# A later place for the merge steps of the next head, and a fixed place in ScalarE's queue for the spread of the inverses

## The chip, the cores and the metric

The kernel runs on one core of one Trainium2 chip. The metric is the device time of one execution in microseconds (us). The engines of the core are TensorE (PE in the profile; PEld is its loading of weights), VectorE (DVE), ScalarE (ACT), GpSimd (POOL) and SyncE (SP). SP issues nearly all the DMAs; each engine takes its own instructions strictly in the order of its queue, so an instruction that waits holds up all that stand behind it.

## The reference

The reference is one layer of a hybrid diffusion backbone: 512 latent tokens and 256 context tokens of 1024 channels go through adaptive normalization, one combined input projection, two token mixers side by side (a bidirectional gated DeltaNet with 8 heads and a bidirectional mLSTM with 4 heads), a gated merge, an output projection, and a gated MLP with a 3x3 convolution. The change touches the DeltaNet alone. Its core is

```
kb = k * beta[..., None]
a_strict = jnp.einsum('bhnld,bhnsd->bhnls', kb, k) * decay
rhs = jnp.concatenate([v * beta[..., None], kb * jnp.exp(gc)[..., None]], axis=-1)
sol = lax.linalg.triangular_solve(a_strict, rhs, left_side=True, lower=True, unit_diagonal=True)
...
def step(s, xc):
    u_n, w_n, kt_n, gt_n = xc[:4]
    v_new = u_n - jnp.einsum('bhld,bhde->bhle', w_n, s)
    s_next = s * gt_n[..., None, None] + jnp.einsum('bhld,bhle->bhde', kt_n, v_new)
    ...
    o = jnp.einsum('bhld,bhde->bhle', qd_n, s) + jnp.einsum('bhls,bhse->bhle', at_n, v_new)
```

For each head, direction and chunk of tokens a triangular system is solved, and then a state of 128x128 is carried from chunk to chunk. The output of a head is normalized over its channels and gated.

## The kernel before, in words

The kernel works with chunks of 128 tokens, so that a head has six chunks (two of context, four of latent tokens) in two directions, which makes twelve triangular matrices. For each it forms the inverse explicitly, and the scan then only multiplies.

**A head passes three stages.** `gdn_prep` projects k, q, v and z of the head (L113 and L114 are the matmuls of all projections), convolves them, forms the triangular matrices (pkk on TensorE, L704 on VectorE) and calls `inverses`. That inverts the 16x16 blocks on the diagonals: the blocks are gathered into cd (L766, L767), written to DRAM and read back in another layout (L768, L769), inverted on GpSimd by a chain of 28 small instructions (L778, L780), written to DRAM again (L782) and read back as cx (L783). L783 waits for L782 to land, and L782 for the last step of the chain.

`merges` builds the whole 128x128 inverse out of these blocks in seven steps, each ended by a `yield`:

1. two DMAs for the decay of the queries (L796), each followed by a product with q on GpSimd (L797; the results are called qs_0 and qs_1); the spread of cx into a block-diagonal U by two ScalarE instructions (L805); a transpose of U on VectorE (L806)
2. y0p, 48 small matmuls (L812), and its copy (L814)
3. w0p (L819), the sum (L821), and eight copies on ScalarE (L823, L825) with eight transposes on VectorE (L824, L826)
4. y1p (L844) and its copy (L846)
5. wp (L852), copies on ScalarE (L856), transposes on VectorE (L857)
6. y2p (L865) and its copy on ScalarE (L867)
7. w2p (L873) and its copies on VectorE (L877)

`gdn_scan` then runs the six chunks of both directions side by side. A chunk has p1 (L911), X (L915, VectorE), p2 (L919), the eviction v3 on ScalarE (L927), p3 (L931) and the new state S (L938, VectorE); in the latent chunks an eviction v2 (L944) and the outputs into a PSUM bank called po (L902) are added. A scan has 16 `yield`s. `gdn_tail` normalizes a finished head: squares of po (L958, ScalarE), a sum (L960), a power on GpSimd that makes the scale fo (L961), and the eviction of po through that scale into o (L964, ScalarE). The bank po is cleared for the next scan by a matmul with zeros (L897), which has to wait until L964 has read it.

**What sets the order.** `mixers` runs the scans s = 0 to 11 (eight DeltaNet heads, four of the mLSTM). At every yield of scan s, `drive` issues what belongs beside it: steps of the tail of head s-1 at the yields in TAIL, the merge steps of head s+1 at the yields in MERGE, and as much of the preparation of a later head as SHARE allots. The framework's scheduler then forms each engine's queue from the order in which the program issues the work, and from its own model of durations. On top of that, `follow(ins, key)` ties an instruction behind the one that `self.anchor[key]` holds at that moment; the keys in use are "t" (matmuls of the scan), "v" (its VectorE work) and "p" (the chain on GpSimd).

Of the kernel before, what the change touches and what calls it, by code (L numbers as in the profile page):

```python
# [12 lines left out]
AF = mybir.ActivationFunctionType  # L13
# [47 lines left out]
LATER = 400  # L61
UP = (0, 9, 13)
XN = 7
MERGE = (1, 2, 4, 6, 8, 10, 11)

DBG = None

# [1 line left out]
class Kern:  # L69
# [716 lines left out]
    def merges(self, h):  # L786

        nc, rot, hold = self.nc, self.rot, self.hold
# [13 lines left out]

        U, UT = (self.gx[:, 2 * G1 + 256 + 384 * i : 2 * G1 + 640 + 384 * i].rearrange("p (c i) -> p c i", i=32) for i in range(2))
        for i in range(2):
            nc.scalar.activation(U[:, :, 16 * i : 16 * i + 16], cx, AF.Copy, scale=self.pm[:, i : i + 1])  # L805
        nc.vector.transpose(UT.rearrange("p c i -> p (c i)"), U.rearrange("p c i -> p (c i)"))  # L806
        yield
        y0p = self.pt([P, NB, 32], "mg", f"y0p{h}")
# [78 lines left out]
    def gdn_scan(self, h):  # L887

        nc = self.nc
        hold, rot, small, tmp = self.hold, self.rot, self.small, self.tmp  # L890
        kT, qT, zs, kt, vt, sc, ssq, Tt, at, _ = self.st[h]
        qs = self.qs[h]
        po = self.pt([P, XC, P], "po", f"po{h}")
        self.po[h] = po
        S = [None, None]
        self.left = 4 * XC
        nc.tensor.matmul(po, self.zero, self.zero.unsqueeze(1).broadcast_to([P, XC, P]), start=True, stop=False)  # L897
        order = [list(range(NCH)), list(range(CC - 1, -1, -1)) + list(range(NCH - 1, CC - 1, -1))]

        def out(x, a, b):  # L900
            self.left -= 1
            nc.tensor.matmul(po[:, x, :], a, b, start=False, stop=self.left == 0)  # L902

        for st in range(NCH):
            cs = [order[d][st] for d in range(2)]
            first = st == 0
            X = [vt[:, c, :] for c in cs]
            if not first:
                p1 = self.pt([P, 2, P], "sc", f"p1_{h}")
                for d, c in enumerate(cs):  # L910
                    g = nc.tensor.matmul(p1[:, d, :], kT[:, c * P : c * P + P], S[d], start=True, stop=True)  # L911
                self.anchor["t"] = g
                for d, c in enumerate(cs):
                    X[d] = tmp.tile([P, P], F32, tag="X", name=f"X{h}")
                    self.anchor["v"] = nc.vector.scalar_tensor_tensor(X[d], p1[:, d, :], self.colA[:, c, 2 + d, h : h + 1], vt[:, c, :], ALU.mult, ALU.subtract)  # L915
                yield
            p2 = self.pt([P, 2, P], "sc", f"p2_{h}")
            for d, c in enumerate(cs):
                g = nc.tensor.matmul(p2[:, d, :], Tt[d][:, c, :], X[d], start=True, stop=True)  # L919
            self.anchor["t"] = g  # L920
            j = 0 if first else 1
            Sn = [None, None]
            if st < NCH - 1:
                v3 = []
                for d, c in enumerate(cs):
                    v3.append(tmp.tile([P, P], F32, tag="v", name=f"v3_{h}", bufs=3))
                    nc.scalar.activation(v3[d], p2[:, d, :], AF.Copy, scale=sc[d][:, 2 + j, c : c + 1])  # L927
                yield
                p3 = self.pt([P, 2, P], "sc", f"p3_{h}")
                for d, c in enumerate(cs):  # L930
                    g = nc.tensor.matmul(p3[:, d, :], kt[:, c, :], v3[d], start=True, stop=True)  # L931
                self.anchor["t"] = g
                for d, c in enumerate(cs):
                    Sn[d] = rot.tile([P, P], F32, tag=f"S{d}", name=f"S{h}_{d}", bufs=2)
                    if first:
                        g = nc.vector.tensor_copy(Sn[d], p3[:, d, :])
                    else:
                        g = nc.vector.scalar_tensor_tensor(Sn[d], S[d], self.ge[:, d, h, c : c + 1], p3[:, d, :], ALU.mult, ALU.add)  # L938
                    self.anchor["v"] = g
            if cs[0] >= CC:  # L940
                for d, c in enumerate(cs):
                    x = c - CC
                    v2 = tmp.tile([P, P], F32, tag="v", name=f"v2_{h}", bufs=3)
                    nc.scalar.activation(v2, p2[:, d, :], AF.Copy, scale=sc[d][:, j, c : c + 1])  # L944
                    out(x, qs[d][:, x * P : x * P + P], S[d])
                    out(x, at[d][:, x, :], v2)
            S = Sn
            yield
# [210 lines left out]
    def mixers(self, e_hc, l1):  # L1159
# [20 lines left out]
        for s in range(GH + MH):  # L1180
# [4 lines left out]
            if s + 1 < GH:  # L1185
                side.append((self.merges(s + 1), MERGE))
            if s in (GH - 1, GH):
# [349 lines left out]
```

## Time and profile before

| | |
|---|---|
| time, median of three runs | 1409.82 us (1408.49 to 1412.16) |
| profiled execution, its time | 1413.52 us |
| profiled execution, its span | 1411.6 us |
| mean granted clock of TensorE | 0.966 |
| TensorE busy | 1326.0 us, 94% |
| VectorE, ScalarE, GpSimd busy | 908.5, 588.5, 507.8 us |
| scans of the eight DeltaNet heads | about 188 to 680 us of the span |

The page of the profile gives for each group of instructions its line, engine, operation, tiles (out<-in), shape, count and times, and the idle time of its engine just before it with the instruction that ended it. A timeline row reads: start, duration, engine, line, operation, tiles, count, and in brackets the idle time before and its releaser. SPq stands for a DMA's issue on SP. Granted clock 1.00 is full speed.

The first L919 with the tile vt is taken as the start of a scan. The starts of scans 0 to 7 lie at 187.79, 249.61, 307.09, 365.47, 425.58, 482.69, 544.55 and 611.50 us.

### The profile page before, as it was taken

What the parts mean: (1) busy time and instruction counts of PE and PEld (TensorE: products, weight loads), DVE (VectorE), ACT (ScalarE), POOL (GpSimd) and SP (SyncE); (2) the same over time, 40 slices, a digit from 0 to 9 for tenths busy, and PEclk for the clock granted to TensorE, in tenths of its full rate; (3) what the DMA queues carried; (4) which work ended last, traced back from release to release, by engine and by line L of the source; (5) the groups of instructions that cost most, each with busy time, mean ns of one, the idle gap of its engine ahead of it and who ended that gap; (6) DMA issues with size and microseconds to landing.
All of it is one profiled execution on the core that took longest, in us unless ns stands there. A gap on an engine that the chain in (4) does not pass through costs nothing. (4 is left out here: it accounts for less than half of the span.)

```text
span 1411.6 us, 24202 instructions
## 1 busy us (share of the span) xinstructions
PE 1326.0 (94%) x9436; PEld 1121.7 (79%) x9436; DVE 908.5 (64%) x1860; ACT 588.5 (42%) x1283; POOL 507.8 (36%) x626
## 2 busy tenths in 40 slices
PE   5888699999999999999899999999989999999997
PEld 4777588878887887889788877788878888888886
DVE  6748973748575774655654464644559879879933
ACT  6555554545555554323233334432234333333331
POOL 4426131130321303243735662000135555555552
PEclk9999799999999999999999999999989999999999
DMA  8633233231322322354524442364323333233321
GB/s 244 152 88 93 56 80 83 74 102 37 89 77 69 82 50 77 106 151 117 144 75 112 114 118 61 98 202 139 126 69 111 90 98 102 84 104 90 104 90 60
DMA packets 233232, 141.85 MB, mean 100 GB/s; under 512 B 32977, under 2 KB 215518, under 8 KB 233118
## 3 DMA queue, kind: packets, MB, share of 16 engines
q1 hardware_dynamic: 233118, 140.31, 35.3%
q8 instruction: 74, 1.21, 0.4%
q14 instruction: 40, 0.33, 0.1%
HBM read 134.47 MB, written 5.82 MB: 99 GB/s over the span
## 5 line engine op out<-in xcount | busy, mean ns | idle before, releaser
L1507 DVE SCALAR_TENSOR_TENSOR y<-pu,fw,y 128x441 f32<-128x441 f32 (+2 forms) x352 | 230.0, 691 | 38.5 <-ACT y L1498 32.9
L137 POOL TENSOR_TENSOR rs<-pw_t,mhalf 128x1 f32<-128x1 f32 x14 | 8.2, 584 | 168.3 <-DVE pw_t L136 168.3
L137 POOL TENSOR_TENSOR kh<-pw_t,phalf 128x6 f32<-128x6 f32 x8 | 11.1, 1390 | 124.1 <-DVE pw_t L136 124.1
L293 POOL TENSOR_TENSOR aw<-aw,sc 128x512 f32<-128x512 f32 x32 | 40.0, 1256 | 31.1 <-DMA aw<-in_w_ada_dram 31.0
L915 DVE SCALAR_TENSOR_TENSOR X<-p,colA,vt 128x128 f32<-128x128 f32 x80 | 24.3, 346 | 33.9 <-PE p L911 33.7
L797 POOL TENSOR_TENSOR qs<-qs,qT 128x512 f32<-128x512 f32 x16 | 20.8, 1304 | 62.2 <-DMA qs<-gd 50.1
L773 POOL MEMSET gx<- 96x16 f32 x8 | 1.0, 123 | 115.4 <-DMA gx<-scr 115.4
L927 ACT ACTIVATE v<-p,sc 128x128 f32<-128x128 f32 x80 | 25.4, 367 | 34.4 <-PE p L919 34.3
L931 PE MATMUL p<-v,kt 128*128 128x128 f32 x160 | 29.8, 302 | 10.5 <-ACT v L927 10.5
L778 POOL TENSOR_TENSOR iv_t<-gx 96x14 f32<-96x14 f32 (+6 forms) x112 | 36.0, 322 | 7.5
L1076 DVE SCALAR_TENSOR_TENSOR C<-C,ge,mpc 128x257 f32<-128x257 f32 x32 | 15.3, 479 | 36.3 <-PE mpc L1072 36.2
L780 POOL TENSOR_TENSOR gx<-gx,iv_t 96x14 f32<-96x14 f32 (+6 forms) x112 | 34.8, 311 | 8.6
L1498 ACT ACTIVATE y<-pu,fw 128x512 f32<-128x512 f32 x44 | 30.0, 683 | 16.1 <-PE pu L114 6.8
L931 PEld LDWEIGHTS p<-v,kt 128*128 128x128 f32 x160 | 23.0, 195 | 16.8 <-ACT v L927 14.9
L646 DVE SCALAR_TENSOR_TENSOR Eg<-Eg,colA,mask 128x128 f32<-128x128 f32 x96 | 33.1, 411 | 3.9 <-DMA Eg<-gd 3.9
L1449 POOL TENSOR_TENSOR al<-y,ah 128x512 fp32r<-128x512 f32 x22 | 28.7, 1304 | 17.3 <-ACT ah L1448 15.8
L1281 DVE SCALAR_TENSOR_TENSOR x<-x,py 128x512 f32<-128x512 f32 x16 | 11.0, 686 | 36.6 <-PE py L114 36.6
L938 DVE SCALAR_TENSOR_TENSOR S<-S,ge,p 128x128 f32<-128x128 f32 x64 | 19.3, 343 | 18.2 <-PE p L931 17.1
L911 PE MATMUL p<-S,kT 128*128 128x128 f32 x160 | 29.9, 289 | 0.0
L944 ACT ACTIVATE v<-p,sc 128x128 f32<-128x128 f32 x64 | 23.1, 378 | 15.8 <-PE p L931 15.0
L1459 DVE TENSOR_TENSOR fd_t<-pd,m 128x512 f32<-128x512 f32 x8 | 5.3, 685 | 37.5 <-PE pd L114 37.5
L598 ACT ACTIVATE cv_t<-cv_y 128x512 f32<-128x512 f32 (+1 forms) x40 | 21.8, 546 | 17.2 <-DVE cv_y L597 14.2
(1235 smaller groups left out, 4699.4 us busy)
## 6 DMA issues: line engine op xcount, KB each, us to landing
aw<-in_w_ada_dram SPq DMA_DIRECT2D x41, 256.0 KB
uw<-in_w_ada_dram SPq DMA_DIRECT2D x16, 512.0 KB
Eg<-gd SPq DMA_DIRECT2D x16, 384.0 KB
gx<-in_w_ada_dram SPq DMA_DIRECT2D x23, 256.0 KB
qs<-gd SPq DMA_DIRECT2D x16, 256.0 KB
xn<-in_x_dram SPq DMA_DIRECT2D x4, 512.0 KB
Em<-r1d SPq DMA_DIRECT2D x8, 256.0 KB
mwo_0r<-in_w_in_dram SPq DMA_DIRECT2D x4, 512.0 KB
```

The costliest lines, as they stand in the source:

```text
L293: eng.tensor_tensor(w, w, self.sc[:, 4 * i : 4 * i + 4, 0:1].broadcast_to([P, 4, P]), ALU.mult)
L646: self.follow(nc.vector.scalar_tensor_tensor(E[:, c, :], E[:, c, :], self.colA[:, c, d, row : row + 1], self.mask[d], ALU.add, ALU.min), "v")
L778: eng.tensor_tensor(t, Bi[:, 0:j, j : j + 1].broadcast_to([8 * NB, j, n]), Bi[:, j : j + 1, j + 1 :].broadcast_to([8 * NB, j, n]), ALU.mult)
L780: g = eng.tensor_tensor(Bi[:, 0:j, j + 1 :], Bi[:, 0:j, j + 1 :], t, ALU.add)
L911: g = nc.tensor.matmul(p1[:, d, :], kT[:, c * P : c * P + P], S[d], start=True, stop=True)
L915: self.anchor["v"] = nc.vector.scalar_tensor_tensor(X[d], p1[:, d, :], self.colA[:, c, 2 + d, h : h + 1], vt[:, c, :], ALU.mult, ALU.subtract)
L927: nc.scalar.activation(v3[d], p2[:, d, :], AF.Copy, scale=sc[d][:, 2 + j, c : c + 1])
L931: g = nc.tensor.matmul(p3[:, d, :], kt[:, c, :], v3[d], start=True, stop=True)
L944: nc.scalar.activation(v2, p2[:, d, :], AF.Copy, scale=sc[d][:, j, c : c + 1])
L1449: nc.gpsimd.tensor_tensor(al[:, j, :], ys[0], ah[:, j, :].bitcast(F32), ALU.subtract)
L1498: nc.scalar.activation(y, ps, AF.Copy, scale=tap(0, 0))
L1507: g = nc.vector.scalar_tensor_tensor(o, u3[:, r0 + dy : r1 + dy, c0 + dx : c1 + dx], tap(dy, dx), o, ALU.mult, ALU.add)
```

## The change

Two edits. MERGE moves the seven merge steps of the next head: the first six each by two yields (from 1, 2, 4, 6, 8, 10 to 3, 4, 6, 8, 10, 12) and the last from 11 to 13. And the two ScalarE instructions that spread the inverses (L805) are tied behind the latest v3 eviction that the scan has issued by then; for this the eviction L927 sets an anchor with the new key "s". The first head's merges run before any scan and have no anchor. The work itself, its instructions and their sizes, is the same.

```diff
-MERGE = (1, 2, 4, 6, 8, 10, 11)
+MERGE = (3, 4, 6, 8, 10, 12, 13)
...
         for i in range(2):
-            nc.scalar.activation(U[:, :, 16 * i : 16 * i + 16], cx, AF.Copy, scale=self.pm[:, i : i + 1])
+            self.follow(nc.scalar.activation(U[:, :, 16 * i : 16 * i + 16], cx, AF.Copy, scale=self.pm[:, i : i + 1]), "s")
...
                     v3.append(tmp.tile([P, P], F32, tag="v", name=f"v3_{h}", bufs=3))
-                    nc.scalar.activation(v3[d], p2[:, d, :], AF.Copy, scale=sc[d][:, 2 + j, c : c + 1])
+                    self.anchor["s"] = nc.scalar.activation(v3[d], p2[:, d, :], AF.Copy, scale=sc[d][:, 2 + j, c : c + 1])
```

On ScalarE at the start of scan 2, before. Here gx is U, cdx holds the inverses, v_2 is the v3 of scan 2, junk with sso the squares of po, Eg a decay table:

```order
L1250 ACTIVATE ge_5_3651<-px_g_5_3658 128x512
L805 ACTIVATE gx<-cdx_3324,pm 128x12x16 x2
L739 ACTIVATE junk,ssq_3641<-ps_tm_q_3636 128x128
L927 ACTIVATE v_2_3702<-p_2_3699,sc_0_2154 128x128
L927 ACTIVATE v_2_3704<-p_2_3699,sc_1_2159 128x128
L739 ACTIVATE junk,ssq_3641<-ps_tm_q_3636 128x128 x2
L958 ACTIVATE junk,sso_3733<-po_2884 128x128 x4
L595 ACTIVATE cv_y<-pc_k_3713,cw 128x256
L964 ACTIVATE o_3745<-po_2884,fo_3742 128x128 x4
```

The same place after the change:

```order
L927 ACTIVATE v_2_3702<-p_2_3699,sc_0_2154 128x128
L927 ACTIVATE v_2_3704<-p_2_3699,sc_1_2159 128x128
L739 ACTIVATE junk,ssq_3641<-ps_tm_q_3636 128x128
L958 ACTIVATE junk,sso_3733<-po_2884 128x128 x4
L595 ACTIVATE cv_y<-pc_k_3713,cw 128x256
L964 ACTIVATE o_3745<-po_2884,fo_3742 128x128 x4
L647 ACTIVATE Eg_0_3776<-Eg_0_3776 128x768
L927 ACTIVATE v_2_3816<-p_2_3813,sc_0_2154 128x128
L927 ACTIVATE v_2_3818<-p_2_3813,sc_1_2159 128x128
L805 ACTIVATE gx<-cdx_3297,pm 128x12x16 x2
```

L805 has gone from ahead of the first pair of v3 to behind the second pair, past the evictions of o. In scans 4 and 6 it is the same; in scans 3 and 5 it stood between L595 and L964 before, and now also stands behind the second pair.

On GpSimd at the end of the inverse chain, around the start of scan 3, before. gx<-gx,iv_t are steps of the chain, qs the decayed queries, fo the scale of o:

```order
L780 TENSOR_TENSOR gx<-gx,iv_t 96x4x11
L797 TENSOR_TENSOR qs_1_3753<-qs_1_3753,qT_3165 128x512
L778 TENSOR_TENSOR iv_t<-gx 96x36
L780 TENSOR_TENSOR gx<-gx,iv_t 96x3x12
L778 TENSOR_TENSOR iv_t<-gx 96x26
L780 TENSOR_TENSOR gx<-gx,iv_t 96x2x13
L778 TENSOR_TENSOR iv_t<-gx 96x14
L780 TENSOR_TENSOR gx<-gx,iv_t 96x14
L797 TENSOR_TENSOR qs_0_4529<-qs_0_4529,qT_3978 128x512
L961 TENSOR_TENSOR fo_4521<-fo_4521,mhalf 128x4
```

And after the change:

```order
L780 TENSOR_TENSOR gx<-gx,iv_t 96x4x11
L778 TENSOR_TENSOR iv_t<-gx 96x36
L780 TENSOR_TENSOR gx<-gx,iv_t 96x3x12
L778 TENSOR_TENSOR iv_t<-gx 96x26
L780 TENSOR_TENSOR gx<-gx,iv_t 96x2x13
L778 TENSOR_TENSOR iv_t<-gx 96x14
L780 TENSOR_TENSOR gx<-gx,iv_t 96x14
L797 TENSOR_TENSOR qs_1_3823<-qs_1_3823,qT_3099 128x512
L797 TENSOR_TENSOR qs_0_4599<-qs_0_4599,qT_3912 128x512
L961 TENSOR_TENSOR fo_4521<-fo_4521,mhalf 128x4
```

The product for qs_1 has left the chain and stands behind its last step; L961 stands behind both products, as it stood behind the one. SP's queue at this place had the DMAs of qs_0, L782 and L783 in this order in scans 3 and 5, and has L782, qs_0, L783 now; in scans 2, 4 and 6 qs_0 stands behind L783 both times.

On VectorE at the end of the preparation, in scan 2, the rows around L767 before:

```order
L713 TENSOR_TENSOR at_1_4205<-pqk_4198,Eg_1_3838 128x512
L766 TENSOR_SCALAR cdx_4138<-cg_4137,pm 128x192
L599 SCALAR_TENSOR_TENSOR vT_4247<-cv_t,cv_y 128x256
L767 SCALAR_TENSOR_TENSOR cdx_4138<-cg_4137,pm,cdx_4138 128x192
L772 MEMSET cg_4137 128x12x16
```

and after the change:

```order
L713 TENSOR_TENSOR at_1_4178<-pqk_4171,Eg_1_3778 128x512
L766 TENSOR_SCALAR cdx_4111<-cg_4110,pm 128x192
L857 STREAM_TRANSPOSE Dm<-gx 32x6x32 x4
L599 SCALAR_TENSOR_TENSOR vT_4214<-cv_t,cv_y 128x256
L767 SCALAR_TENSOR_TENSOR cdx_4111<-cg_4110,pm,cdx_4111 128x192
L772 MEMSET cg_4110 128x12x16
```

The four transposes of merge step 5 have come between the two instructions that fill cd. Before, they stood ahead of the whole group, ahead of L704.

## The prediction

> **What bounds the kernel now.** I read the page first, then TensorE's waits in the part where the eight DeltaNet scans run, then the timelines around the starts of two scans.
>
> ```profile
> span 1411.6 us, 24202 instructions
> PE 1326.0 (94%) x9436; PEld 1121.7 (79%) x9436; DVE 908.5 (64%) x1860; ACT 588.5 (42%) x1283; POOL 507.8 (36%) x626
> ...
> PE p L931 <- ACT v L927: 10.5, 6, 3.3
> PE po L897 <- ACT o L964: 2.7, 2, 1.6
> ```
>
> TensorE works 94% of the span, so the end is set by the amount of its work, by its gaps and by its granted clock. The change alters no matrix product; it can win only gaps and clock. Between 130 and 560 us (the last two rows: total, times, longest) there are six waits of L931 for the eviction v3 (L927) and two of L897 for o (L964), 13.2 us in all; they stand at the start of scans 0 and 2 to 6. The even scans 2, 4 and 6 look like this (scan 2, which starts at 307.09):
>
> ```profile
> 307.25 0.32 SPq L782 DMA_DIRECT2D scx<-gx  x1
> 309.40 0.67 SPq L796 DMA_DIRECT2D qs<-gd  x1
> 311.74 0.80 ACT L805 ACTIVATE gx<-cdx,pm 128x192 f32<-128x192 f32 x2 [3.32 <-DMA cdx<-scx]
> 313.10 0.79 PE L931 MATMUL p<-v,kt 128*128 128x128 f32 x2 [3.30 <-ACT v L927]
> 313.54 1.26 POOL L797 TENSOR_TENSOR qs<-qs,qT 128x512 f32<-128x512 f32 x1 [6.32 <-DMA qs<-gd]
> 318.16 1.13 ACT L964 ACTIVATE o<-po,fo 128x128 f32<-128x128 f32 x4
> 323.86 0.39 PE L897 MATMUL po<-zero 128*128 128x512 bf16 x1
> ```
>
> The spread of the inverses (L805) is ahead of the scan's first v3 in ScalarE's queue and waits for a DMA, and v3 (L927) runs behind it, and TensorE waits 3.30 us at L931. In scans 3 and 5 the same L805 stands one place later, ahead of o (scan 3, start 365.47):
>
> ```profile
> 365.47 0.61 PE L919 MATMUL p<-vt,gx 128*128 128x128 f32 x4
> 368.48 0.33 SPq L796 DMA_DIRECT2D qs<-gd  x1
> 371.25 0.32 SPq L782 DMA_DIRECT2D scx<-gx  x1
> 371.84 1.29 POOL L797 TENSOR_TENSOR qs<-qs,qT 128x512 f32<-128x512 f32 x1 [0.62 <-DMA qs<-gd]
> 373.10 1.06 POOL L961 TENSOR_TENSOR fo<-fo,mhalf 128x4 f32<-128x4 f32 x1
> 375.41 0.80 ACT L805 ACTIVATE gx<-cdx,pm 128x192 f32<-128x192 f32 x2 [3.67 <-DMA cdx<-scx]
> 376.12 1.12 ACT L964 ACTIVATE o<-po,fo 128x128 f32<-128x128 f32 x4
> 377.29 0.38 PE L897 MATMUL po<-zero 128*128 128x512 bf16 x1 [1.55 <-ACT o L964]
> 378.28 0.74 PE L931 MATMUL p<-v,kt 128*128 128x128 f32 x4 [0.61 <-ACT v L927]
> ```
>
> After a gap the clock is often granted low for a while. Columns: window, its length, TensorE busy, granted clock, DMA share, GB/s.
>
> ```profile
> 312.00:318.00 6.00, 4.90 (x62) 0.50 0.45 135
> 376.00:382.00 6.00, 4.09 (x19) 1.00 0.01 3
> 431.00:435.00 4.00, 3.77 (x43) 0.57 0.68 210
> 494.00:500.00 6.00, 5.28 (x17) 0.72 0.00 0
> 549.00:555.00 6.00, 5.54 (x116) 0.72 0.44 137
> ```
>
> Busy time times what the clock lacks is 2.45 us in scan 2, 0 in scan 3, 1.6 in scan 4, 1.5 in scan 5, 1.55 in scan 6: about 7 us. With the 13.2 us of idle time, **about 20 us hang on these starts**; that is the most that can be won.
>
> **The change, part by part.** (1) *L805 goes behind the second pair of v3.* In the even scans the first L931 finds its v3 at once. In scan 0, whose gap is quoted next, that is the whole effect.
>
> ```profile
> 190.97 0.49 PE L931 MATMUL p<-v,kt 128*128 128x128 f32 x2 [0.79 <-ACT v L927]
> 431.23 0.65 PE L931 MATMUL p<-v,kt 128*128 128x128 f32 x2 [2.94 <-ACT v L927]
> 494.11 0.38 PE L897 MATMUL po<-zero 128*128 128x512 bf16 x1 [1.17 <-ACT o L964]
> 549.46 0.49 PE L931 MATMUL p<-v,kt 128*128 128x128 f32 x2 [2.20 <-ACT v L927]
> ```
>
> What is late next is o. TensorE's own work from the scan's start to L897 is 10.3 us in scan 3 (377.29 less 1.55, from 365.47). For scan 2 I estimate 9 us, since its L897 stands at 323.86, and the 16.8 us from the start hold 3.3 idle, the block y0p, which now comes later (about 2 us), and some 2.5 lost to the clock. Until now scan 2's head gap hid that o comes late: L964 ran only at 318.16. In the changed order o hangs on POOL: L961, which computes o's scale, stands behind the two products with qs (L797), and these stand behind the last step of the inverse chain.
>
> (2) *The merge steps stand two yields later.* So qs_1's product, which used to run inside the inverse chain, three steps before its end, comes after it. This takes one product of 1.3 us out of the chain. Against it the chain starts later: the four transposes L857 now stand between L766 and L767, which feeds the chain, and VectorE is without a gap there; and ScalarE's eight copies L823 and L825 now run after the third v3, ahead of the norms of the next head.
>
> ```profile
> 276.49 1.57 DVE L857 STREAM_TRANSPOSE Dm<-gx 32x192 f32<-32x192 f32 x4
> 326.84 0.36 ACT L823 COPY gx<-gx 32x192 f32<-32x192 f32 x1 [2.17 <-DVE gx L821]
> 328.96 0.34 ACT L825 COPY Dm<-gx 32x192 f32<-32x192 f32 x1
> 335.96 1.04 ACT L102 CAST wz4h<-wz4r 128x1024 fp32r<-128x1024 f32 x1 [0.82 <-PE px_q L113]
> ```
>
> The transposes cost 1.57 us. The copies take 2.5 us (326.84 to 329.30); 0.82 of that fits into ScalarE's idle time before L102, and 1.3 us of L856's copies leave the same stretch, so 0.4 us is left. 1.57 + 0.4 - 1.3: **the chain ends about 0.7 us later** against its scan. Its bounds: -1.3 (if the later start is hidden) and +2 (if the copies find no idle time).
>
> (3) *The qs DMAs.* In scans 3 and 5 the one for qs_0 is now queued on SP behind L782, which waits for the chain's end; before, it was issued 2.8 us ahead of it. In the even scans it stands behind L783 as before.
>
> *Even scans.* From L782 to the end of o: 2.15 us until the DMA's issue (309.40 - 307.25), 4.14 to the product (313.54 - 309.40), 1.26, then L961 1.06 and L964 1.12: 9.7 us. L782 stood at +0.16, -0.15 and -0.82 us from the scan's start, its first L919 (rows of scans 4, 6 and 5 below); 0.7 later, o ends at 10.6, 10.3 and 9.6 us after the start, against TensorE's arrival at about 9. So it waits 1.6, 1.3 and 0.6 us at L897, and then 0.6 each at L931 as in scan 3, since Eg (L647) and the second v3 follow o on ScalarE: 5.3 us in place of 3.30 + 2.94 + 2.20 = 8.4. Gain 3.1 us. The clock: the split gap of scan 5 (1.17 + 0.6) cost 1.5, that of scan 3 none; I take 1 us each, 3 in place of 5.6. Gain 2.6.
>
> ```profile
> 425.43 0.32 SPq L782 DMA_DIRECT2D scx<-gx  x1
> 425.58 0.38 PE L919 MATMUL p<-vt,Bt 128*128 128x128 f32 x2
> 543.73 0.32 SPq L782 DMA_DIRECT2D scx<-gx  x1
> 544.55 0.38 PE L919 MATMUL p<-vt,gx 128*128 128x128 f32 x2
> 482.69 0.50 PE L919 MATMUL p<-vt,gx 128*128 128x128 f32 x3
> 487.78 0.32 SPq L782 DMA_DIRECT2D scx<-gx  x1
> 489.31 1.29 POOL L797 TENSOR_TENSOR qs<-qs,qT 128x512 f32<-128x512 f32 x1 [1.55 <-DMA qs<-gd]
> ```
>
> *Scans 3 and 5.* From L782: 0.32 its issue, 3.4 to 3.6 for the qs_0 DMA (368.48 to 371.84; scan 5 the same way), 1.29, 1.06, 1.12: 7.2 to 7.4 us. L782 stood 5.78 and 5.1 us after the start; with 0.7 more, o ends at 13.7 and 13.2 us instead of 11.8 and 11.4. TensorE waits 1.85 us longer in each: **a loss of 3.7 us**, and 2.5 us of clock, since a gap of 3 us cost 1.6 to 2.5 above and these had 0 and 1.5.
>
> *Within the scans* the small matmuls of the merges stand at other places. L823 and L764 now come between evictions that TensorE wants: up to two 1.4-us groups of copies a scan, 0 at the low end, 1.3 us a scan at the high end; nearest to these is the 0.82 us that ScalarE has idle there, so I take half a microsecond in six scans: 3 us.
>
> *The sum:* -0.8 (scan 0) - 3.1 - 2.6 + 3.7 + 2.5 + 3 = +2.7 us on the profiled execution's 1413.5, which makes 1416. That execution is 3.7 above the median of 1409.8, so on the scale of the median the sum is **1412.5 us**. It moves by about 8 us for each microsecond of the chain's end (five starts, and the clock with them).
>
> The Trainium skill, TensorE: Matmul & The Clock Gate, Part 1, says that the clock falls to half after an idle window of about 3.4 us, and that the window runs freely. By that rule the even starts, whose gap is now cut in two, would lose nothing to the clock (a gain of 5.6 us, not 2.6), and neither would scans 3 and 5 (a gain of 1.5, not a loss of 2.5); the sum would be -4.3, a time of 1405.5 us, at the edge of faster. The trace differs on the length (0.72 after a gap of 2.20 us) and agrees that like gaps fare unlike (1.00 in scan 3, 0.72 in scan 5); the 0.07 of faster within the forecast, below, covers this case.
>
> **The rivals.** *All starts become free.* If the chain ends 1.3 us earlier instead of 0.7 later and o is ready, the even scans keep no gap, scan 3 and 5 gain a little: 8.4 + 5.6 + 0.8 and about 1 us, 16 us, so 1394; with all 20, 1390. For it: L805 leaves the way of v3, and qs_1 leaves the chain. Against it: L961 behind two products, on one queue.
>
> *Slower: POOL's and SP's queue decide.* If the chain ends 2 us later, o is late by 1.3 us more in each of five scans, with 0.6 us of clock for each microsecond: 10 to 11 us, and 1.3 us within each scan instead of 0.5 adds 5. The sum is 1428; it is slower by the bound from a shift of about 0.9 us on. For it: every step from L782 to L964 is in order and has a quoted length. Against it: VectorE has idle time earlier in the scan.
>
> *The order does not matter.* Gaps only change place, because the inverses set the pace of the scans: then the starts cost the same 20 us and the time is 1410. That is within my forecast's own reach.
>
> **How the numbers follow.** About 0.3% (4.2 us) can be told from no change here. Forecast, a trade that nearly cancels: 0.42, with 1403 to 1420 its own range; free starts 0.27; slower 0.25; only the place of the gaps 0.06 (counted with no change). Of the forecast's 0.42 I give 0.07 to faster, 0.20 to same, 0.15 to slower. Faster is then 0.34, same 0.26, slower 0.40. The range is 1394 to 1426; it leaves out the best of the free starts and the worst of the queue.
>
> **What would show it.** Right: L931's first wait is gone in scans 2, 4 and 6; L897's wait for o appears there, at 0.6 to 1.6 us, and grows to about 3.4 in scans 3 and 5; L961 starts less than 0.1 us after the qs_0 product; L805 never stands ahead of a v3; granted clock near 1 after the even starts. Wrong: no wait of L897 in the even scans (the chain was early), waits over 2 us there (it was later than 0.7), or a change of more than 5 us after 620 us, where nothing is expected.

## The result and the profile after

The changed kernel takes **1389.23 us** (median of five, 1388.90 to 1390.91) against 1409.82 us: a ratio of 0.9861, 95% interval 0.9843 to 0.9878. A second measurement gave 1392.51 us beside 1409.29 us for the kernel before, a ratio of 0.9876 (0.9861 to 0.9891). So it is faster by about 17 to 21 us. The forecast was no change (1412.5 us, 1394 to 1426), so the time lies below its range; it is about the time that the rival "all starts become free" gave (1394, and 1390 at the most).

The page of the changed kernel, its rows on the span, TensorE and the granted clock by slices:

```profile
span 1389.3 us, 24222 instructions
PE 1313.7 (95%) x9436; PEld 1109.1 (80%) x9436; DVE 908.8 (65%) x1860; ACT 589.3 (42%) x1283; POOL 509.3 (37%) x626
PEclk9999799999999999999999999999999999999999
```

TensorE's waits between 130 and 560 us, where 13.2 us stood for L931 and L897 before:

```profile
PE w0p L819 <- DVE y L814: 11.0, 1, 11.0
PE p L931 <- ACT v L927: 1.6, 3, 0.6
PE p L911 <- DVE S L936: 1.1, 1, 1.1
PE po L897 <- ACT o L964: 0.9, 1, 0.9
```

2.5 us are left, and TensorE keeps its clock behind them. From the start of scan 0 to that of scan 7, before and after (length, TensorE busy, granted clock, DMA share, GB/s):

```profile
187.79:611.50 423.71, 410.08 (x4471) 0.98 0.30 80
187.91:595.03 407.12, 403.39 (x4471) 1.00 0.31 83
```

**The stretch of the scans**, as these two rows have it, is used below beside the times. It is 611.50 - 187.79 = 423.7 us before and 595.03 - 187.91 = 407.1 us after: 16.6 of the 22.3 us by which the two spans differ. The rest of the span was 987.9 and 982.2 us here, and in eight more profiled executions below, of kernels that leave the first head's preparation alone, it was anywhere from 982.5 to 988.7 us, with no order by kernel (the changed kernel's second one: 985.0); the work there is nearly the same in all of them, and its granted clock is not. So I take 16.6 us as the change's own, and leave the other 5.7 to single executions; the medians of the second measurement differ by 16.8 us. One of the forecast's signs of being wrong, more than 5 us of change after 620 us, came with it: from the start of scan 7 to the end the first pair of traces differs by 5.8 us, the changed kernel's second trace by 4.0; the clock behind the scans, given at the end of the experiments, is enough to make that difference.

**Where the 16.6 us came from** shows at the start of scan 3, which the forecast expected to become slower. After the change it starts at 357.96:

```profile
341.63 0.94 SPq L631 DMA_DIRECT2D Eg<-gd  x2
344.85 0.37 SPq L768 DMA_DIRECT2D scr<-cdx  x1
347.49 0.32 SPq L769 DMA_DIRECT2D gx<-scr  x1
360.58 0.32 SPq L782 DMA_DIRECT2D scx<-gx  x1
360.99 0.38 SPq L796 DMA_DIRECT2D qs<-gd  x1
349.55 0.12 POOL L773 MEMSET gx<- 96x16 f32 x1 [14.52 <-DMA gx<-scr]
364.49 1.29 POOL L797 TENSOR_TENSOR qs<-qs,qT 128x512 f32<-128x512 f32 x1 [2.27 <-DMA qs<-gd]
365.73 1.06 POOL L961 TENSOR_TENSOR fo<-fo,mhalf 128x4 f32<-128x4 f32 x1
366.82 1.15 ACT L964 ACTIVATE o<-po,fo 128x128 f32<-128x128 f32 x4 [2.69 <-POOL fo L961]
369.01 0.75 PE L931 MATMUL p<-v,kt 128*128 128x128 f32 x4 [0.61 <-ACT v L927]
```

L782 stands 2.6 us after the scan's start; it was 5.8 before and was to be 6.5. The order of the queue behind it is as predicted (qs_0 behind L782, L961 directly behind qs_0's product), but it starts 3.9 us earlier than predicted, and o is done 10.0 us after the start, when TensorE has just arrived. In scan 2 L782 went from 0.16 us after the start to 4.0 us before it. **The inverse chain ends 2.5 to 4.2 us earlier against its scan** (2.5 us in scan 5, 4.2 in scans 2 and 4). In scan 3, where it is 3.2 us, three things make this up. The same instructions of the kernel before, with the start at 365.47:

```profile
351.04 0.94 SPq L631 DMA_DIRECT2D Eg<-gd  x2
352.52 0.37 SPq L768 DMA_DIRECT2D scr<-cdx  x1
357.04 0.32 SPq L769 DMA_DIRECT2D gx<-scr  x1
359.36 0.12 POOL L773 MEMSET gx<- 96x16 f32 x1 [14.17 <-DMA gx<-scr]
```

From L768 to L773, the blocks' trip through DRAM to GpSimd, it was 6.84 us and is 4.70: 2.1 us. From L773 to L782, the chain itself, it was 11.89 (359.36 to 371.25) and is 11.03: 0.9 us, since qs_1's product has left it. And L768 starts 13.11 us ahead of the scan in place of 12.95: 0.2 us. In the other scans the trip became 1.3 to 2.4 us shorter, and the chain about 1.0. The trip is the part that the forecast did not have. Its second half, L769 to L773, hardly changed (2.32 and 2.06 us); the first, L768 to L769, went from 4.52 to 2.64 us. Ahead of L768 on SP stand the two loads of the next decay table, Eg: 1.5 us ahead before, 3.2 us now. They wait for the last reader of the table's buffer, L713, which stands just ahead of L766 on VectorE, and L768 waits for L767. Between these two L857 now takes its 1.57 us:

```profile
351.52 0.31 DVE L766 TENSOR_SCALAR cdx<-cg,pm 128x192 f32<-128x192 f32 x1
352.08 0.42 DVE L767 SCALAR_TENSOR_TENSOR cdx<-cg,pm,cdx 128x192 f32<-128x192 f32 x1
```

```profile
342.12 0.32 DVE L766 TENSOR_SCALAR cdx<-cg,pm 128x192 f32<-128x192 f32 x1
342.46 1.57 DVE L857 STREAM_TRANSPOSE Dm<-gx 32x192 f32<-32x192 f32 x4
344.06 0.43 DVE L599 SCALAR_TENSOR_TENSOR vT<-cv_t,cv_y 128x256 f32<-128x256 f32 x1
344.40 0.41 DVE L767 SCALAR_TENSOR_TENSOR cdx<-cg,pm,cdx 128x192 f32<-128x192 f32 x1
```

(The first fence is the kernel before, the second the changed one.) L766 ran 13.95 us ahead of the scan and now runs 15.84 ahead: the whole group from L704 on became 1.9 us earlier, for the most part because L857, 1.57 us, no longer stands in front of it. The 1.57 us of L857 between L766 and L767 take back most of that, and give Eg's loads the lead.

In the even scans not all of this reaches o. There qs_0's DMA stands behind L783, which waits for L782 to land, and in the changed kernel that takes 3.7 to 4.7 us where it took 1.7 (414.42 to 419.09 in scan 4). So o is done 7.7, 9.8 and 8.9 us after the starts of scans 2, 4 and 6, where the forecast said 10.6, 10.3 and 9.6; only in scan 4 does TensorE, which arrives at about 9, still wait for it (0.9 us).

### The profile page after: what moved, and what is told of

Read it like the earlier page. It is cut to its first block, busy times and chain, and to the rows that moved or that the text cites. A ratio compares the mean times of both kernels' runs of the same rounds, so it can differ in the third digit from the quotient of the medians.

```text
span 1389.3 us, 24222 instructions
## 1 busy us (share of the span) xinstructions
PE 1313.7 (95%) x9436; PEld 1109.1 (80%) x9436; DVE 908.8 (65%) x1860; ACT 589.3 (42%) x1283; POOL 509.3 (37%) x626
## 5 line engine op out<-in xcount | busy, mean ns | idle before, releaser
L773 POOL MEMSET gx<- 96x16 f32 x8 | 1.0, 125 | 116.9 <-DMA gx<-scr 116.9
L927 ACT ACTIVATE v<-p,sc 128x128 f32<-128x128 f32 x80 | 25.4, 370 | 40.5 <-PE p L919 40.3
L1447 DVE TENSOR_TENSOR y<-y,y 128x512 f32<-128x512 f32 x22 | 28.5, 1296 | 0.9
L911 PE MATMUL p<-S,kT 128*128 128x128 f32 x160 | 27.7, 288 | 1.1 <-DVE S L936 1.1
L902 PE MATMUL po<-v,at 128*128 128x128 f32 x128 | 26.6, 290 | 1.1 <-ACT v L944 1.1
L931 PE MATMUL p<-v,kt 128*128 128x128 f32 x160 | 25.8, 283 | 1.6 <-ACT v L927 1.6
```

The costliest lines, as they stand in the source:

```text
L1447: nc.vector.tensor_tensor(ys[0], ys[0], ys[1], ALU.mult)
```

## The experiments

The theories in the expectations: A, the end of the inverse chain against its scan decides the starts; B, L805's place in ScalarE's queue does; C, the trip through DRAM was slow because of Eg's loads; D, small matmuls in pieces cost TensorE time. D came from these rows, y0p's matmuls over the whole program in the kernel before and in the changed one (count, busy time, mean ns). A head's 48 of them show as 96 records:

```profile
L812 PE MATMUL y0p<-gx,cg 32*32 32x32 f32 x768 | 11.7, 200 | 0.0
```

```profile
L812 PE MATMUL y0p<-gx,cg 32*32 32x32 f32 x768 | 8.4, 193 | 0.0
```

### The new MERGE alone

```diff
-            self.follow(nc.scalar.activation(U[:, :, 16 * i : 16 * i + 16], cx, AF.Copy, scale=self.pm[:, i : i + 1]), "s")
+            nc.scalar.activation(U[:, :, 16 * i : 16 * i + 16], cx, AF.Copy, scale=self.pm[:, i : i + 1])
```

> The change's MERGE alone, L805 not tied. In the even scans L805 then still stands ahead of the first v3 (L927). Theory A (the new MERGE ends the inverse chain 3 to 4 us earlier against its scan; that is most of the gain): the inverses land about 2.6 us after the scan's start instead of 4.6, L931 waits 0.5 to 1.3 us in scans 2, 4 and 6 instead of 2.2 to 3.3, and the time is 1392 to 1397. Theory B (L805's place in ScalarE's queue is the cause): the waits stay at 2 to 3 us and the time is 1404 to 1410.

It took 1410.88 us, ratio 0.9999 (0.9974 to 1.0023); the stretch of the scans is 424.4 us. This edit alone wins nothing, about as theory B said. L805 stands ahead of the first v3 in scans 2, 4 and 6, and here is scan 2, which starts at 311.08:

```profile
313.50 0.45 ACT L805 ACTIVATE gx<-cdx,pm 128x192 f32<-128x192 f32 x1 [1.79 <-DMA cdx<-scx]
314.34 0.44 ACT L805 ACTIVATE gx<-cdx,pm 128x192 f32<-128x192 f32 x1
314.93 0.62 ACT L927 ACTIVATE v<-p,sc 128x128 f32<-128x128 f32 x2
```

The inverses land 2.4 us after the start, as theory A said, in place of 4.65; but the wait of L931 only falls to 2.23 us (2.48 and 2.30 in scans 4 and 6), since the two halves of L805 still come first, and another activation (L1250) has come between them. In scans 3 and 5 the waits do go, from 2.2 and 1.8 us to 0.7 and 0.6, without the tie. But y0p is in more pieces than before, and is busy for 12.9 us; what the pieces cost is taken up below.

### The tie of L805 alone

```diff
-MERGE = (3, 4, 6, 8, 10, 12, 13)
+MERGE = (1, 2, 4, 6, 8, 10, 11)
```

> L805 tied behind the latest v3, MERGE as before. L805 then stands behind the first pair of v3, ahead of the squares of po and of o. Theory A: the chain ends where it did before (L782 about 0.2 us after the start of scan 2 and 5.8 us after that of scan 3), the wait of L931 for the first v3 goes and a wait of L897 for o of 1 to 2.5 us comes in the even scans; 1402 to 1408. Theory B: all starts of the even scans are free and the time is 1392 to 1397.

1398.11 us, ratio 0.9916 (0.9884 to 0.9948); the stretch is 413.3 us. This lies between the two expectations. The chain ends where it did (L782 0.17 us after the start of scan 2, 5.78 after that of scan 3), as theory A needs, and scans 3 and 5 keep their waits. But the waits of L897 in the even scans did not come, because with the old MERGE y0p stands ahead of L897 and waits itself, for the transpose behind L805:

```profile
PE y0p L812 <- DVE gx L806: 3.6, 3, 1.5
PE po L897 <- ACT o L964: 2.9, 2, 1.7
PE p L931 <- ACT v L927: 1.7, 4, 0.6
```

3.6 us for y0p in place of 8.4 us for v3, and short gaps in place of long ones. So the tie alone is worth 10.4 of the 16.6 us, and the new MERGE, worth nothing alone, is worth the other 6.2 with it (413.3 to 407.1 us in the stretch): it takes away this wait of y0p and the late o of scans 3 and 5.

### y0p in one block, in the new MERGE alone and in the kernel before

```diff
                 g = nc.tensor.matmul(y0p[r, c, :], X[r, c, :], UT[r, c, :], start=True, stop=True, tile_position=(r.start, r.start))
+                self.follow(g) if h else None
```

> The run with the new MERGE alone, and y0p's 48 small matmuls tied behind the scan's latest matmul, so that they stand as one block as in the changed kernel, and not in pieces between full-size matmuls. Theory D (small matmuls in pieces cost TensorE time: y0p was busy 11.7 us there for 672 matmuls against 7.1 in the changed kernel): y0p falls to about 7 us and the time from 1411 to 1404 to 1407, with the waits for v3 unchanged at 2.2 to 2.5 us. Without theory D (the pieces only show slow clock and waits): 1409 to 1413.

1404.69 us, ratio 0.9944 (0.9913 to 0.9975); stretch 414.3 us in place of 424.4, y0p 8.4 us. The waits for v3 are as they were (2.2 to 2.5 us). Its times lay far apart, 1398 to 1407 us.

> The kernel before with y0p's 48 small matmuls tied into one block, and nothing else. Theory D: y0p's busy time falls from 11.7 to about 8.4 us over the eight heads, the waits at the scan starts stay as they were (3.3, 2.9, 2.2 and about 2), time 1404 to 1407. Without theory D: 1408 to 1412.

1401.55 us, ratio **0.9943** (0.9926 to 0.9961); stretch 419.6 in place of 423.7. That is below the 1404 to 1407 expected. The waits at the starts stayed (L931 10.9 us in all, L897 2.9). The order of TensorE has 22 pieces of y0p in the kernel before, 9 in this one and 9 in the changed one; 4.1 us over 13 pieces are 0.3 us for each piece more. The place after the first p1 of scan 0 shows it, before and in one block:

```profile
193.56 0.38 PE L812 MATMUL y0p<-gx,cg 32*32 32x32 f32 x20
193.86 0.71 PE L911 MATMUL p<-S,kT 128*128 128x128 f32 x4
194.50 0.67 PE L812 MATMUL y0p<-gx,cg 32*32 32x32 f32 x54
195.10 0.50 PE L113 MATMUL px_v<-hx,wv2h 128*128 128x512 f32 x1
```

```profile
194.06 0.60 PE L911 MATMUL p<-S,kT 128*128 128x128 f32 x4
194.59 1.02 PE L812 MATMUL y0p<-gx,cg 32*32 32x32 f32 x96
195.54 0.50 PE L113 MATMUL px_v<-hx,wv2h 128*128 128x512 f32 x1
```

96 small matmuls in one block take 0.95 us (194.59 to 195.54), so 74 of them would take 0.73; in two pieces 74 take 0.90 (0.30 and 0.60), and the four of L911 between them 0.64 in place of 0.53. The Trainium skill, TensorEngine Tiling (Array Packing), Key Properties, says that a change of the tiling mode drains TensorE; it gives no price, and these rows are one.

So one block alone is worth 4 us of the stretch (and 8 us of the time, by the medians), and the change brings it by its side. But the change also cuts other groups up: in the stretch of the scans y0p goes from 20 pieces to 7, w2p (L873) from 8 to 19 and wp (L852) from 19 to 29. The following table counts every place where a matmul on TensorE has another tile shape (32x32, 64x64 or 128x128) than the one before it. It splits the stretch of each trace into TensorE's idle time, by scan; what the clock took, which is busy time times what the clock lacks, in windows of 2 us; and the rest, which is TensorE's work at full speed, with whatever short waits show as busy.

| kernel | stretch | idle, scan 0 | idle, scans 2, 4, 6 | idle, scans 3, 5 | clock | rest | changes of shape |
|---|---|---|---|---|---|---|---|
| before | 423.7 | 0.9 | 8.4 | 4.3 | 7.8 | 402.3 | 172 |
| before, y0p in one block | 419.6 | 1.5 | 8.3 | 4.6 | 6.7 | 398.5 | 144 |
| new MERGE alone | 424.4 | 2.1 | 7.0 | 1.3 | 3.4 | 410.7 | 230 |
| new MERGE, y0p in one block | 414.3 | 1.3 | 7.1 | 1.2 | 1.5 | 403.3 | 180 |
| tie alone | 413.3 | 1.8 | 4.9 | 4.1 | 3.3 | 399.1 | 150 |
| both edits | 407.1 | 1.2 | 1.5 | 1.0 | 0.0 | 403.4 | 184 |

The rest follows the changes of shape through all six kernels, by about 0.14 us for each (12.2 us for the 86 between the lowest and the highest); a piece more makes two of them, which fits the 0.3 us above. The changed kernel has 12 more than the kernel before, and its rest is 1.1 us longer, not shorter: what it wins at y0p it loses again at w2p and wp.

### Eg's loads behind the blocks' trip

```diff
-            self.nc.sync.dma_start(E.rearrange("p c t -> p (c t)"), self.gd[0, row, d : d + 1, :].broadcast_to([P, NALL]))
+            self.queue_after(self.nc.sync.dma_start(E.rearrange("p c t -> p (c t)"), self.gd[0, row, d : d + 1, :].broadcast_to([P, NALL])), getattr(self, "back", None))
...
-        nc.sync.dma_start(Bi, scr.rearrange("c b j i -> (c b) j i"))
+        self.back = nc.sync.dma_start(Bi, scr.rearrange("c b j i -> (c b) j i"))
```

> The kernel before, with the two loads of the next decay table (Eg, 384 KB each) queued on SP behind L769 instead of ahead of L768. Theory C (the round trip of the blocks through DRAM is slow because it shares the DMA engines with Eg's loads): L768 to L769 falls from 4.4 to about 2.6 us and the chain starts 2 us earlier; waits at the scan starts fall by 1.5 to 2 us each, time 1396 to 1402. If the round trip has its length from elsewhere: L768 to L769 stays above 4 us and the time is 1407 to 1411.

1412.47 us, ratio 1.0014 (0.9994 to 1.0034). The trip did fall (L768 to L769 2.5 us), but scan 0 starts 5 us later, at 192.78, since the loads of the first heads were held up too. The stretch of the scans is 421.5 us, only 2.2 shorter.

> The changed kernel with Eg's loads queued behind L769 too. Its starts have 2.5 us of waits left in all. Theory C: L768 to L769 stays at about 2.6 us, since Eg's loads are already 3 us ahead there; the time is 1387 to 1390. Without theory C the same; a time over 1392 would mean that Eg then comes late for its own reader.

1396.21 us, ratio 0.9892 (0.9856 to 0.9928): the time went up and not down, by the same 5 us ahead of scan 0 (193.13). The stretch of the scans is 406.0 us, about as in the changed kernel, and L768 to L769 2.6 us: here Eg's loads had already been out of the way.

The third run ties only the loads of heads 4 to 7 (`self.back if row > 3 else None`), and stands on the kernel before.

> The kernel before with Eg's loads behind L769, but only for heads 4 to 7, whose loads stand beside scans, so that the first heads' preparation is not held up (in the earlier run with all heads it was, by about 5 us). Theory C: L768 to L769 2.6 us in scans 2 to 5, waits of the even scans 1.3 to 1.9 us (3.3 and 2.9 before), those of scans 3 and 5 3.9 us as in that run, since qs_0 is behind L782 on SP there; time 1404 to 1408.

1412.04 us, ratio 1.0006 (0.9990 to 1.0023): no gain, where 1404 to 1408 was expected. The stretch is 424.4 us. SP in scan 1, GpSimd and TensorE at the start of scan 3 (362.21):

```profile
289.08 0.37 SPq L768 DMA_DIRECT2D scr<-cdx  x1
291.66 0.33 SPq L769 DMA_DIRECT2D gx<-scr  x1
292.04 0.90 SPq L631 DMA_DIRECT2D Eg<-gd  x2
...
370.88 2.71 POOL L797 TENSOR_TENSOR qs<-qs,qT 128x512 f32<-128x512 f32 x1 [4.30 <-PE p L919]
...
375.79 0.38 PE L897 MATMUL po<-zero 128*128 128x512 bf16 x1 [3.31 <-ACT o L964]
376.78 0.84 PE L931 MATMUL p<-v,kt 128*128 128x128 f32 x4 [0.61 <-ACT v L927]
```

L768 to L769 is 2.58 us with the loads behind (4.43 with them ahead), so theory C holds for the length of the trip. The Trainium skill, DMA: Bandwidth & Descriptors, Queues, rings and completion order, says that one engine's DMAs share one row of rings and are consumed in ring order; the trace agrees. But the gain did not reach the time. Scan 2 waits 1.45 us in place of 3.30; scans 4 and 6 2.20 and 2.61, little changed. And in scans 3 and 5 the scheduler now put qs_0's DMA behind L782, and o came late: 3.3 + 0.6 us of waiting where 1.55 + 0.61 had been. That is the loss that the forecast expected of the change (1.85 us in each of these scans), seen where the chain ended 4.4 us after the start; in part it is another thing, as qs_0's product took 2.71 us there and not 1.29. The chain itself, L773 to L782, was also longer in scan 3 than before (12.8 us against 11.9).

### The changed kernel with a longer chain

```diff
-            eng.tensor_tensor(t, Bi[:, 0:j, j : j + 1].broadcast_to([8 * NB, j, n]),
+            for _ in range(5 if j == 7 else 1): eng.tensor_tensor(t, Bi[:, 0:j, j : j + 1].broadcast_to([8 * NB, j, n]),
```

> The changed kernel with one multiplication of the inverse chain done five times instead of once (1.5 us more on GpSimd); the scheduler then also puts qs_1's product back into the chain (1.3 us more). Nothing else is changed. Theory A: the chain ends 2.5 to 3 us later, waits at L897 come back (1 to 2.5 us in scans 3 to 6) and with them the low clock; time 1398 to 1406. If the chain's end does not set the starts: 1389 to 1392.

1401.05 us, ratio 0.9920 (0.9895 to 0.9946): 9 to 12 us slower than the changed kernel, and theory A holds for the even scans. The stretch of the scans is 415.2 us, 8 more; scan 0 starts 3.6 us later, since the first heads' chains are longer too. SP in scan 2 (start 309.56), then TensorE at the starts of scans 2 and 4:

```profile
309.12 0.32 SPq L782 DMA_DIRECT2D scx<-gx  x1
...
319.67 0.38 PE L897 MATMUL po<-zero 128*128 128x512 bf16 x1 [1.17 <-ACT o L964]
320.66 0.64 PE L931 MATMUL p<-v,kt 128*128 128x128 f32 x3 [0.61 <-ACT v L927]
...
436.31 0.58 PE L897 MATMUL po<-zero 128*128 128x512 bf16 x1 [2.93 <-ACT o L964]
437.31 1.01 PE L931 MATMUL p<-v,kt 128*128 128x128 f32 x3 [0.41 <-ACT v L927]
```

L782 is 3.6 us later against scan 2 than in the changed kernel, and in the even scans the waits come that the forecast expected of a late chain, in kind if not in size: 1.2 + 0.6 us here, 2.9 + 0.4 and 1.2 in scans 4 and 6, where it had 1.6, 1.3 and 0.6, each with 0.6 more. Scans 3 and 5 did not suffer, though the chain ended 5.7 and 5.6 us after their starts: the scheduler put qs_0's DMA ahead of L782 again, and one wait of 0.6 us was left in each.

### L961 ahead of qs_0's product, and the first head's y0

```diff
-            nc.gpsimd.tensor_tensor(x, x, qT, ALU.mult)
+            self.follow(nc.gpsimd.tensor_tensor(x, x, qT, ALU.mult), "f" if d == 0 else "none")
...
-        nc.gpsimd.tensor_tensor(f, f, self.mhalf[:, 0:XC], ALU.pow)
+        self.anchor["f"] = nc.gpsimd.tensor_tensor(f, f, self.mhalf[:, 0:XC], ALU.pow)
```

> The changed kernel with qs_0's product tied behind L961 on GpSimd, so that the scale of o no longer waits for qs_0's DMA and product. 2.5 us of waits at L897 and L931 are left in scans 3 to 5. Theory A: L961 runs 2 to 3 us earlier, these waits go, and the time is 1385 to 1388. If they have another cause: 1388.5 to 1391.

1391.59 us, ratio 0.9854 (0.9836 to 0.9872). Of the waits of L897 and L931 at the starts two of 0.2 us are left, and the stretch is 404.5 us, 2.6 less than in the changed kernel. The time does not show it. Beside the changed kernel itself:

> The changed kernel once more, for comparison on the same chip: 1388 to 1391, and a second trace of it, which shows whether the lower loss to the clock after the scans (about 7 us against 14 in the trace before) belongs to the change or to one execution.

> The changed kernel with qs_0's product behind L961 once more, against the changed kernel on the same chip. Its scans took 2.6 us less in the trace, its time did not show it: 1386 to 1388 if the waits were worth what they lasted, 1389 to 1391 if not.

The changed kernel took 1392.51 us there (stretch 407.3 us, the rest 985.0), and with L961 first 1391.89 us, ratios 0.9876 (0.9861 to 0.9891) and 0.9869 (0.9852 to 0.9886): the same, as far as these times tell. The stretch was again shorter, 404.4 us; the rest of the span was 988.3. A gain of 2.5 us is smaller than what the rest varies by. The second trace of the changed kernel loses 8.5 us to the clock behind the scans (busy time times what the clock lacks, in windows of 2 us), where its first lost 6.7 and the kernel before 14.4; the other kernels' traces lose 6 to 11. So the large difference in the first pair of traces belongs mostly to one execution.

The last run adds ScalarE as the engine that copies y0 for the first head, whose merges run before any scan:

```diff
-        nc.vector.tensor_copy(y0, y0p)
+        (nc.vector.tensor_copy if h else nc.scalar.copy)(y0, y0p)
```

> As the run before, and the first head's copy of y0p (L814) made by ScalarE instead of VectorE, where it stands behind the gates of the other mixer and TensorE waits 11 us for it in every kernel so far. If ScalarE is free there, the wait goes and 4 to 8 us are won (1380 to 1384), less the part that comes back as a longer wait of y1p for VectorE's transposes; if the wait only moves on to y1p, 1386 to 1390.

**1388.08 us**, ratio 0.9851 (0.9836 to 0.9866), 4.4 us below the changed kernel's beside it; the two intervals just overlap, so it is probably faster, and not surely. TensorE's waits between 130 and 190 us:

```profile
PE y1p L844 <- DVE Dm L824: 6.0, 2, 5.1
PE w0p L819 <- ACT y L814: 3.6, 1, 3.6
PE wp L852 <- DVE y L846: 1.2, 1, 1.2
```

The wait of 11.0 us for y0 fell to 3.6, and more than half of the gain came back as longer waits for VectorE in the next two steps. TensorE's idle time from 130 us to the first scan is 11.0 us, and 13.8 in the changed kernel beside it.

## Why the prediction was wrong

**What bounds the kernel** was right: the gaps at the starts of the scans and the clock behind them, about 20 us, were what could be won, and they are what was won: of the 21.4 us of idle time and clock in the first row of the table 17.7 went. With 1394, and 1390 at the most, the rival of the free starts gave the time, and nearly by its mechanism; its condition, a chain that ends 1.3 us earlier, was more than met, o was just in time, and scans 3 and 5 gave 5 us and not 1.

**The step that failed** is "the chain ends about 0.7 us later", with its terms 1.57 + 0.4 - 1.3. The runs show 2.5 to 4.2 us earlier.

- The 1.57 us of L857 were counted where they arrived and not where they left. Ahead of L704 they had held up the same group, with L767 in it; L766 ran 1.9 us earlier. The order of before and after was in the text, and said that they had stood "ahead of L704".
- The 0.4 us of the copies L823 and L825 was not seen: the group on VectorE came earlier, not later.
- qs_1's product leaving the chain was right in kind, and brought 0.9 to 1.1 us of the chain's length and not 1.3.
- The trip through DRAM was missing. It was taken as a constant behind L768, though the DMA in front of it on SP was to move with another reader. It became 2.1 us shorter in scan 3, and the runs with Eg's loads behind L769 show that these loads set its length. This is the term that no row of VectorE or GpSimd could give.

Its lower bound, -1.3, was therefore no bound either. Term by term, forecast and measured in the stretch of the scans (us, rounded):

| term | forecast | measured |
|---|---|---|
| wait in scan 0 | -0.8 | +0.3 |
| waits, scans 2, 4, 6 | -3.1 | -6.9 |
| their clock | -2.6 | -6.2 |
| waits, scans 3, 5 | +3.7 | -3.3 |
| their clock | +2.5 | -1.7 |
| within the scans | +3 | +1.1 |
| sum | +2.7 | -16.6 |

The greatest error is in scans 3 and 5: o ends 10.0 and 9.7 us after their starts, and not 13.7 and 13.2. In scans 4 and 6 the forecast of o was off by less than a microsecond, but for a reason that cancels: the chain ended far earlier, and "from L782 to the end of o: 9.7 us" became 13.2 to 14.1 (11.7 in scan 2), in large part since the inverses' own trip back, L782 to L783, took 3.7 to 4.7 us in place of 1.7. This constant was the second step that did not hold.

**The slope was too steep.** The forecast said about 8 us for each microsecond of the chain's end. With the chain's end 3.0 to 4.0 us later the stretch grew by 8 us in all: only the three even scans suffered, and there o became later by only 1.2 to 2.4 us, since the trip from L782 to L783 was short again. That the queue behind L782 sets when o is done was right; only, after the change this queue begins in time.

**"Within the scans" 3 us of loss** came out as 1.1, and not by the way forecast. The small matmuls did change their places, as the forecast said; this was costed by ScalarE's copies, and the pieces themselves at nothing. With y0p in one block both times, the new MERGE adds 4.8 us to TensorE's rest (398.5 to 403.3 us in the table) and the block takes away 3.8 (402.3 to 398.5). So one kind of piece nearly paid for the other. Another loss, the wait of 1.1 us for S at L911, came in scan 0.

**The clock.** The 3 us that the forecast still charged to the even scans, and the 2.5 more for scans 3 and 5, were not lost: no gap at a start is longer than 0.89 us after the change, and none of them cost clock. What a gap of 2 us costs stays uncertain in a single case: in the new MERGE alone the gap of 2.48 us in scan 4 cost nothing, and those of 2.23 and 2.30 in scans 2 and 6 1.7 us each. Over all traces here, 17 of 20 gaps of 2.2 to 3.3 us at the starts were followed by a low clock. The Trainium skill's window of about 3.4 us (TensorE: Matmul & The Clock Gate, Part 1) is too long for these gaps; that it runs freely fits the difference between like ones, and perhaps the wide spread of the kernels that have them (1398 to 1407 us for one of them, 1388.9 to 1390.9 for the changed kernel in its first runs).

**What the two edits do** is told by the rows of the table. The tie takes L805 out of the way of v3: the idle time of the even scans falls from 8.4 to 4.9 us, and what is left there is mostly y0p's own wait for the transpose; scans 3 and 5 keep theirs. MERGE alone leaves L805 in the way and adds changes of shape, which eat its gain; but the chain ends early with it, and scans 3 and 5 lose their waits (4.3 to 1.3 us). Together, y0p stands behind L805 and L897 and does not wait, and o is in time or nearly so in all five scans. Of the 16.6 us, 9.9 are idle time and 7.8 clock, less 1.1 for the changes of shape.

## What to carry to other kernels

When an instruction moves along a queue, count it at both ends: those that it now precedes become later, those that it preceded become earlier, and so do the DMAs that wait for them. A small DMA on the critical chain (96 KB here) can take its length from the transfer just ahead of it on its queue; look at what stands there, and whether the change moves that. And count in how many pieces all groups of small-tile matmuls stand between full-size ones, not only the group that you look at: each piece cost here, though no wait showed it.

## What the runs showed of the hardware

- A piece more of 32x32 matmuls between full-size ones cost about 0.3 us (4.1 us for 13 pieces), with no idle time shown on TensorE. Over six kernels a change of tile shape from one matmul to the next cost about 0.14 us (12.2 us for 86).
- After a gap of 2.2 to 3.3 us on TensorE at the start of a scan the clock was low 17 times out of 20, for 1.6 to 3.2 us of lost work in the 9 us behind it; after a gap of 1.15 to 1.9 us 4 times out of 15 (these 4, and some of the others, had a second gap of 0.6 us just behind); after shorter ones, the longest 1.11 us, never.
- A DMA of 96 KB (the blocks, L768 to L769) took 2.5 to 2.6 us with 768 KB of loads (Eg) queued behind it, and 4.3 to 4.5 us when they had been issued 1.5 us ahead of it on the same queue. In the changed kernel the trip back fares alike: L782 to L783 takes 2.9 to 4.7 us (360.58 to 363.75 in scan 3) where it took 1.7 to 2.0, and a load of 512 KB (L94) is issued 1.65 us ahead of L782 there; no run moves that load, so that it is the cause is not shown. The spread L805 no longer awaits the inverses, but in the even scans qs_0's DMA does stand behind L783, and the wait of 0.9 us in scan 4 hangs on it.
- What lies outside the stretch of the scans, nearly the same work, took 982 to 989 us from one execution to another; the clock lost 6 to 15 us behind the scans alone. A change of two or three microseconds in this kernel has to be read from a stage and not from the time.
